# The first load of a batched matrix product, taken in three loads of 2, 2 and 4 rows per partition

## Chip, cores and metric

The kernel runs on one core of one Trainium2 chip. The metric is the time of one execution in microseconds (us), as the device measures it. It is some 1.8 us longer than the span of the profile, which runs from the first to the last instruction.

## The reference

32 products of a 256 x 512 matrix with a 512 x 384 matrix, in float32:

```python
x: (32, 256, 512) float32      y: (32, 512, 384) float32
np.einsum('bij,bjk->bik', x, y)    # (32, 256, 384) float32
```

That is 41.94 MB to read and 12.58 MB to write.

## The kernel before

A load of x brings four batches (a "q") at once: 32 partitions per batch and eight neighbouring rows of x on each partition, so 16 KB in one piece per partition. A unit (a "u") is two batches; its y comes in two loads with 6 KB per partition. All loads and stores are issued by SP, in the order of the program.

```python
    def load_x(q):                                    # P = 128, R = 8 rows, J = 512
        x_of[q] = x_pool.tile([P, R, J], F32, name="x_sb")
        keep(nc.sync.dma_start(
            out=x_of[q],
            in_=x[q * Q : (q + 1) * Q].rearrange("g (p r) j -> (g p) r j", r=R)))

    def transpose(q, half):
        ...
        for t in range(half * NJ // 2, (half + 1) * NJ // 2):     # NJ = 4
            for e in range(0, NE, 2):                             # NE = 4
                t_ps = tpsum_pool.tile([P, 2, H, Q * PQ], F32, name="t_ps")
                for f in range(2):
                    for h in range(H):                            # H = 2
                        keep(nc.tensor.transpose(
                            t_ps[:, f, h], x_sb[:, h * NE + e + f, t::NJ], identity))
                ...                                   # DVE and ACT in turn round t_ps to float16

    for s in range(U + 2):                            # U = 16 units
        if s + ahead < U:
            load(s + ahead)                           # ahead = 2; unit 0 and 1 are loaded before the loop
        if s == 0:
            transpose(0, 0); transpose(0, 1)
        if s >= 2:
            collect(s - 2)                            # PSUM -> SBUF
        if 1 <= s <= U:
            multiply(s - 1)                           # 32 matmuls
        if s < U:
            round_y(s)                                # y to float16
        ...                                           # the transposes of later x, in halves
        if s >= 2:
            store(s - 2)
```

The first tile t_ps takes row 0 and then row 4 of each partition (`h * NE + e + f`), then rows 1 and 5.

Of the kernel before, what the change touches and what calls it, by code (L numbers as in the profile page):

```python
# [1 line left out]

# [5 lines left out]


MM_DT = mybir.dt.float16  # L10
F32 = mybir.dt.float32
P = 128


Q = 4
G = 2

LAG = 4


@with_exitstack
def kernel(
    ctx: ExitStack,
    tc: tile.TileContext,
    x: bass.AP,
    y: bass.AP,
    out: bass.AP,
):
    nc = tc.nc

    B, I, J = x.shape
    _, _, K = y.shape


    M = P // G
    NE = I // M
    NJ = J // P



    PQ = P // Q
    R = I // PQ
    H = R // NE
    U = B // G

    const_pool = ctx.enter_context(tc.tile_pool(name="const", bufs=1))
    x_pool = ctx.enter_context(tc.tile_pool(name="x_pool", bufs=3))
    y_pool = ctx.enter_context(tc.tile_pool(name="y_pool", bufs=5))
    yr_pool = ctx.enter_context(tc.tile_pool(name="yr_pool", bufs=2))
    xt_pool = ctx.enter_context(tc.tile_pool(name="xt_pool", bufs=2))  # L50
    o_pool = ctx.enter_context(tc.tile_pool(name="o_pool", bufs=5))
    tpsum_pool = ctx.enter_context(tc.tile_pool(name="tpsum", bufs=4, space=bass.MemoryType.PSUM))
    opsum_pool = ctx.enter_context(tc.tile_pool(name="opsum", bufs=4, space=bass.MemoryType.PSUM))


    keep = tc.keep_in_program_order

    identity = const_pool.tile([P, P], F32)
    make_identity(nc, identity)

    x_of, y_of, yr_of, xt_of, ps_of, o_of = {}, {}, {}, {}, {}, {}

    def load_x(q):
        x_of[q] = x_pool.tile([P, R, J], F32, name="x_sb")
        keep(
            nc.sync.dma_start(
                out=x_of[q],
                in_=x[q * Q : (q + 1) * Q].rearrange("g (p r) j -> (g p) r j", r=R),
            )
        )  # L70

    def load(u):

        if u == 0:
            load_x(0)
        if (u + 1) * G % Q == 0 and u + 1 < U:
            load_x((u + 1) * G // Q)
        y_of[u] = y_pool.tile([P, G, NJ, K], F32, name="y_sb")
        for g in range(G):
            keep(  # L80
                nc.sync.dma_start(
                    out=y_of[u][:, g],
                    in_=y[u * G + g].rearrange("(q t) k -> q t k", q=P),
                )
            )

    def transpose(q, half):

        x_sb = x_of[q]
        if half == 0:  # L90
            xt_of[q] = xt_pool.tile([P, NJ, NE, Q * PQ, H], MM_DT, name="xt_sb")
        n = 0
        for t in range(half * NJ // 2, (half + 1) * NJ // 2):
            for e in range(0, NE, 2):
                t_ps = tpsum_pool.tile([P, 2, H, Q * PQ], F32, name="t_ps")
                for f in range(2):
                    for h in range(H):
                        keep(
                            nc.tensor.transpose(  # L99
                                t_ps[:, f, h], x_sb[:, h * NE + e + f, t::NJ], identity  # L100
                            )
                        )
                dst = xt_of[q][:, t, e : e + 2].rearrange("c f p h -> c f h p")
                if n % 2 == 0:
                    keep(nc.vector.tensor_copy(dst, t_ps))  # L105
                else:
                    keep(nc.scalar.copy(dst, t_ps))  # L107
                n += 1

    def round_y(u):  # L110
        y_sb = y_of.pop(u)
        yr_of[u] = yr_pool.tile([P, G, NJ, K], MM_DT, name="y_r")
        for g in range(G):
            for t in range(NJ):
                if t % 2 == 0:
                    keep(nc.scalar.copy(yr_of[u][:, g, t], y_sb[:, g, t]))  # L116
                else:
                    keep(nc.vector.tensor_copy(yr_of[u][:, g, t], y_sb[:, g, t]))  # L118

    def multiply(u):  # L120
        xt_sb, y_r = xt_of[u * G // Q], yr_of.pop(u)
        ps_of[u] = []
        for e in range(NE):
            o_ps = opsum_pool.tile([P, K], F32, name="o_ps")
            ps_of[u].append(o_ps)
            for t in range(NJ):
                for g in range(G):
                    a = (u * G + g) % Q
                    keep(
                        nc.tensor.matmul(  # L130
                            o_ps[g * M : (g + 1) * M],
                            xt_sb[:, t, e, a * PQ : (a + 1) * PQ].rearrange("c p h -> c (p h)"),
                            y_r[:, g, t],
                            start=(t == 0),
                            stop=(t == NJ - 1),
                        )
                    )

    def collect(u):
        o_of[u] = o_pool.tile([P, NE, K], F32, name="o_sb")  # L140
        for e in range(NE):
            if e % 2 == 0:
                keep(nc.scalar.copy(o_of[u][:, e], ps_of[u][e]))  # L143
            else:
                keep(nc.vector.tensor_copy(o_of[u][:, e], ps_of[u][e]))  # L145
        del ps_of[u]

    def store(u):
        keep(
            nc.sync.dma_start(  # L150
                out=out[u * G : (u + 1) * G].rearrange("g (m e) k -> (g m) e k", e=NE),
                in_=o_of.pop(u),
            )
        )


    ahead = LAG - 2
    for u in range(ahead):
        load(u)
    for s in range(U + 2):  # L160
        if s + ahead < U:
            load(s + ahead)
        if s == 0:
            transpose(0, 0)
            transpose(0, 1)
        if s >= 2:
            collect(s - 2)
        if 1 <= s <= U:
            multiply(s - 1)
        if s < U:  # L170
            round_y(s)
        for half in range(2):
            q = (s + 1 - half) * G // Q
            if (s + 1 - half) * G % Q == 0 and 0 < q < B // Q:
                transpose(q, half)
        if s >= 2:
            store(s - 2)


# [1 line left out]
_INS = ['x', 'y']  # L181
_OUTS = [((32, 256, 384), 'float32')]


# [23 lines left out]
```

## Time and profile before

| | before |
|---|---|
| time | 136.07 us (median of 3; 135.93 to 136.09) |
| span of the profile | 134.3 us |
| busy: PE, ACT, DVE | 66%, 48%, 42% of the span |
| transfers | 56: 8 of x, 32 of y, 16 of the output |
| mean rate | 406 GB/s over the span, 422 in the steady part |
| first transposes, first multiply, first store issued | 8.72, 15.91, 23.92 us |

The prediction below shows the slices and the chain. Here are the page's lines on transfers (DMA): how many packets, their sizes, and the queues that they came from with packets, MB and share of the 16 DMA engines' time.

```profile
DMA packets 8073, 54.65 MB, mean 407 GB/s; under 512 B 896, under 2 KB 896, under 8 KB 7040
q1 hardware_dynamic: 8064, 54.53, 97.8%
q8 instruction: 6, 0.10, 0.3%
q14 instruction: 3, 0.02, 0.0%
```

Queue q1 is the kernel's own loads and stores and fills 97.8% of the engines' time. The two queues called "instruction" I take for reads of the program itself: where `pool_fetch` below adds 1024 instructions, eight more reads of 8 KB stand there. They are 0.3% in all.

### The profile page before, as it was taken

Reading aid. Unit: us, or ns where it says so; the run is one execution under the profiler, and the core shown is the slowest. Engines: PE = TensorE matmul, PEld = TensorE weight load, DVE = VectorE, ACT = ScalarE, POOL = GpSimd, SP = SyncE. Lnnn points to the kernel's source line nnn. Section 1 sums busy time; section 2 is a strip of 40 time slices with the busy share of each in tenths; the row PEclk is TensorE's granted clock in tenths of the full one; section 3 lists DMA queues with packets and bytes.
Section 4 is the critical chain, followed back from the end, with each engine's and each line's share of the span. In section 5 each row is a group of like instructions: output and inputs, shape, how many; then the busy total and the mean of one; then the engine's idle time right before and its main releaser. Section 6 shows DMA issues by size and latency. Waiting matters only on the chain.

```text
span 134.3 us, 1968 instructions
## 1 busy us (share of the span) xinstructions
PE 88.5 (66%) x768; PEld 73.2 (55%) x768; DVE 56.2 (42%) x128; ACT 63.9 (48%) x129; POOL 0.7 (1%) x6
## 2 busy tenths in 40 slices
PE   0049494979299767786099771976439986597920
PEld 0049474768177666666078661864427665476810
DVE  0004717471743365711634318460363425628620
ACT  3004837662762476712744428560475336738610
POOL 2000000000000000000000000000000000000000
PEclk9999999999959999999968999999965899779997
DMA  5999999999999999999999999999999999999993
GB/s 112 415 400 450 409 417 421 456 388 421 417 448 408 409 428 421 457 394 417 413 443 436 408 417 428 442 422 402 425 423 444 426 402 427 419 427 419 417 394 158
DMA packets 8073, 54.65 MB, mean 407 GB/s; under 512 B 896, under 2 KB 896, under 8 KB 7040
## 3 DMA queue, kind: packets, MB, share of 16 engines
q1 hardware_dynamic: 8064, 54.53, 97.8%
q8 instruction: 6, 0.10, 0.3%
q14 instruction: 3, 0.02, 0.0%
HBM read 41.94 MB, written 12.58 MB: 406 GB/s over the span
## 4 chain that ended last, share of the span: by engine, by line
DMA 78%; PE 13%; ACT 4%; DVE 0%; issue 0%
DMA y_sb<-in_y_dram 40%; DMA x_sb<-in_x_dram 38%; PE o_ps L130 9%; PE t_ps L99 3%; ACT xt_sb L107 2%; ACT y_r L116 1%; ACT o_sb L143 1%; DVE o_sb L145 0%
## 5 line engine op out<-in xcount | busy, mean ns | idle before, releaser
L130 PE MATMUL o_ps<-y_r,xt_sb 128*64 128x384 f16 x512 | 52.4, 364 | 28.5 <-ACT o_sb L143 20.8
L130 PEld LDWEIGHTS <-xt_sb 128*64 128x64 f16 x512 | 39.1, 121 | 38.8 <-issue 22.4
L116 ACT CAST y_r<-y_sb 128x384 f16<-128x384 f32 x64 | 29.5, 514 | 38.7 <-DMA y_sb<-in_y_dram 38.6
L99 PE MATMUL t_ps<-identity,x_sb 128*128 128x128 f32 x256 | 36.9, 301 | 11.4 <-DMA x_sb<-in_x_dram 11.4
L99 PEld LDWEIGHTS t_ps<-identity,x_sb 128*128 128x128 f32 x256 | 34.1, 211 | 16.0 <-issue 16.0
L118 DVE CAST y_r<-y_sb 128x384 f16<-128x384 f32 x64 | 20.0, 356 | 46.7 <-DMA y_sb<-in_y_dram 46.7
L107 ACT CAST xt_sb<-t_ps 128x512 f16<-128x512 f32 x32 | 22.4, 731 | 23.6 <-PE t_ps L99 23.6
L105 DVE CAST xt_sb<-t_ps 128x512 f16<-128x512 f32 x32 | 22.6, 728 | 24.1 <-PE t_ps L99 23.8
L145 DVE COPY o_sb<-o_ps 128x384 f32<-128x384 f32 x32 | 16.3, 544 | 2.1 <-PE o_ps L130 2.1
L143 ACT COPY o_sb<-o_ps 128x384 f32<-128x384 f32 x32 | 13.9, 492 | 1.3 <-PE o_ps L130 1.3
L107 ACT ACT_TABLE_LOAD x1 | 1.3, 1283 | 0.7 <-PEq L192 0.7
masks.py:199 POOL TENSOR_SCALAR_AFFINE_SELECT identity<-identity 128x128 f32<-128x128 f32 x1 | 0.3, 294 | 0.1
masks.py:197 POOL MEMSET identity<- 128x128 f32 x1 | 0.2, 206 | 0.3 <-POOLq L192 0.3
L192 POOL MEMSET const-bfloat16-1.0<- 128x1 bf16 x1 | 0.1, 102 | 0.0
L192 POOL MEMSET const-uint8-127<- 128x1 uint8 x1 | 0.1, 102 | 0.0
L192 POOL MEMSET const-float32-0.0<- 128x1 f32 x1 | 0.1, 99 | 0.2 <-issue 0.2
L192 POOL MEMSET const-float32-1.0<- 128x1 f32 x1 | 0.1, 99 | 0.0
## 6 DMA issues: line engine op xcount, KB each, us to landing
y_sb<-in_y_dram SPq DMA_DIRECT2D x32, 768.0 KB, 17.9
x_sb<-in_x_dram SPq DMA_DIRECT2D x8, 2048.0 KB, 20.8
out_dram<-o_sb SPq DMA_DIRECT2D x16, 768.0 KB, 17.8
```

Source lines behind the costliest of these rows:

```text
L99: nc.tensor.transpose(t_ps[:, f, h], x_sb[:, h * NE + e + f, t::NJ], identity)
L105: keep(nc.vector.tensor_copy(dst, t_ps))
L107: keep(nc.scalar.copy(dst, t_ps))
L116: keep(nc.scalar.copy(yr_of[u][:, g, t], y_sb[:, g, t]))
L118: keep(nc.vector.tensor_copy(yr_of[u][:, g, t], y_sb[:, g, t]))
L130: nc.tensor.matmul(o_ps[g * M : (g + 1) * M], xt_sb[:, t, e, a * PQ : (a + 1) * PQ].rearrange("c p h -> c (p h)"), y_r[:, g, t], start=(t ...
L143: keep(nc.scalar.copy(o_of[u][:, e], ps_of[u][e]))
L145: keep(nc.vector.tensor_copy(o_of[u][:, e], ps_of[u][e]))
L192: nc = _bacc.Bacc("TRN2", target_bir_lowering=False, num_devices=1)
```

## The change

The intent: transposes of the first rows can start while the later rows still arrive.

```diff
+FIRST = (0, 2, 4, 8)
 ...
     def load_x(q):
         x_of[q] = x_pool.tile([P, R, J], F32, name="x_sb")
-        keep(nc.sync.dma_start(
-            out=x_of[q],
-            in_=x[q * Q : (q + 1) * Q].rearrange("g (p r) j -> (g p) r j", r=R)))
+        src = x[q * Q : (q + 1) * Q].rearrange("g (p r) j -> (g p) r j", r=R)
+        cuts = FIRST if q == 0 else (0, R)
+        for k, r in enumerate(cuts[:-1]):
+            rows = slice(r, cuts[k + 1])
+            keep(nc.sync.dma_start(out=x_of[q][:, rows], in_=src[:, rows]))
```

More of the change, by code (lines that the diff above doesn't have):

```diff
@@ L64, in load_x @@
         x_of[q] = x_pool.tile([P, R, J], F32, name="x_sb")
-        keep(
-            nc.sync.dma_start(
-                out=x_of[q],
-                in_=x[q * Q : (q + 1) * Q].rearrange("g (p r) j -> (g p) r j", r=R),
-            )
-        )
+        src = x[q * Q : (q + 1) * Q].rearrange("g (p r) j -> (g p) r j", r=R)
[3 more added lines that the diff above has]
+            keep(nc.sync.dma_start(out=x_of[q][:, rows], in_=src[:, rows]))
     def load(u):
```

## The prediction

Passages of the prediction, and one of the expectation of `pool_fetch`, that rested on what no run of this case shows are cut, and the cuts are marked. The sum of the prediction came to +0.1 us. Its one term other than zero, +0.1 us for the 18 added packets of each engine, is among the cuts, so the line of the sum stands without the estimate behind it.

> **What bounds the kernel now.** I read the page's slices first, then the chain that ended last, then windows of 16 us, then the order of events on the load-issuing engine and on the compute engines in the first 30 us and the last 20 us. The slices show that transfers never pause:
>
> ```profile
> PE   0049494979299767786099771976439986597920
> DMA  5999999999999999999999999999999999999993
> HBM read 41.94 MB, written 12.58 MB: 406 GB/s over the span
> ```
>
> The DMA engines are full (9) in 38 slices of 40, while PE is at 66% of the span and DVE and ACT are under 50%. The chain that ended last agrees: DMA has 78% of it and PE 13%. The steady rate comes from the windows (columns: length, four busy engines and POOL, granted clock, DMA share, GB/s):
>
> ```profile
> 24.40:40.40 16.00, 12.47 (x113) 10.20 (x110) 7.57 (x18) 8.98 (x19) 0.00 (x0) 0.90 1.00 419
> 56.40:72.40 16.00, 10.00 (x85) 8.05 (x86) 5.68 (x15) 6.96 (x15) 0.00 (x0) 0.89 1.02 424
> 88.40:104.40 16.00, 9.98 (x80) 7.59 (x80) 5.72 (x15) 7.01 (x15) 0.00 (x0) 0.82 1.02 426
> ```
>
> The six windows from 24.4 to 120.4 us show 419, 423, 424, 425, 426 and 416 GB/s, a mean of 422. The kernel's 54.53 MB at that rate take 129.2 us. The span is 134.3 us, so only 5.1 us are not steady streaming. Most of that is the start: two-microsecond windows show 98 and 213 GB/s up to 4 us, so 0.62 MB, worth 1.5 us; about 2.5 us are lost there. At the end, after 132 us, nearly nothing moves (59 GB/s), about 2.0 us lost to the landing of the last store. The rest is 0.35 us of lower rate between 128 and 132 us (381 and 390 GB/s) and some 0.2 us between 4 and 8 us.
>
> The start on the compute side, which the change aims at:
>
> ```profile
> 8.60 0.33 SPq L66 DMA_DIRECT2D x_sb<-in_x_dram  x1
> 8.72 6.00 PE L99 MATMUL t_ps<-identity,x_sb 128*128 128x128 f32 x32 [8.72 <-DMA x_sb<-in_x_dram]
> 15.91 0.32 PE L130 MATMUL o_ps<-y_r,xt_sb 128*64 128x384 f16 x1 [1.19 <-ACT y_r L116]
> 19.15 0.63 DVE L118 CAST y_r<-y_sb 128x384 f16<-128x384 f32 x2 [3.11 <-DMA y_sb<-in_y_dram]
> 21.04 0.63 DVE L118 CAST y_r<-y_sb 128x384 f16<-128x384 f32 x2 [1.25 <-DMA y_sb<-in_y_dram]
> 23.92 0.35 SPq L150 DMA_DIRECT2D out_dram<-o_sb  x1
> ```
>
> PE waits 8.7 us for the first load, transposes for 6.0 us, multiplies from 15.9 us, and then DVE idles 3.11 us until the second unit's y lands at 19.15 and 21.04 us. That landing, not the first transposes, holds back what follows. At the end:
>
> ```profile
> 115.54 4.47 PE o_ps L130 x32
> 120.02 2.15 PE t_ps L99 x16
> 122.16 0.02 issue
> 122.19 0.74 ACT xt_sb L107
> 122.92 0.09 issue
> 123.01 5.41 PE o_ps L130 x64
> 128.42 0.02 issue
> 128.44 0.56 DVE o_sb L145
> ```
>
> The last 64 matmuls end at 128.4 us, the last store is issued at about 129.1 and takes 4.4 us (the shortest landing of a store). The store queue is almost empty by then. So the end is both things at once: the stream of transfers, and a compute tail that starts from the last loads. Both hang on when the loads arrive.
>
> [...] 896 packets are under 512 B, and 56 transfers times 16 are 896.
>
> **The change part by part.** The first 2 MB load becomes three: rows 0-1 (0.52 MB), rows 2-3 (0.52 MB) and rows 4-7 (1.05 MB) of each partition. All bytes, all arithmetic and the order of the transfers stay.
>
> Packets: the page counts 8064 in the queue: 896 semaphore writes, 6144 of 6 KB (48 y loads and stores times 128) and so 1024 for the eight x loads, 128 of 16 KB each. The first load then has 3 times 128, which is 256 more, and 32 more semaphore writes: 288 more, 18 per engine. [...]
>
> Issue time: an issue of a load takes 0.33 to 0.63 us on the issuing engine. Two more, at about 0.4 us, end the third piece's issue near 2.0 us instead of 1.1 and push the next by about 0.8 us. By 4 us only 0.62 MB have moved, so the first piece still keeps the engines occupied when the others are queued: hidden, 0 us.
>
> Waits of the issuing engine: in the built kernel each transfer from the ninth on waits for the one eight places earlier. Every later transfer and the one it waits for shift by two places alike, so those waits stay the same, with the third piece in the place of the whole load. Only the two y loads of the third unit, which waited for nothing (they were among the four issues from 2.78 to 4.82 us), now wait for the first and second pieces. From the cumulated GB/s, 0.52 MB have moved by about 3.7 us and 1.05 MB by about 5.0; the whole load's 2.10 MB are reached at 7.7 and it landed at 8.6, so add 0.9: landings near 4.6 and 5.9 us. Those y loads follow 7.34 MB in the queue, whose turn ends near 2.5 + 7.34/0.422 = 19.9 us. The later issue has over 13 us of slack: 0 us.
>
> Compute: the built order on PE keeps its 32 transposes in the same order and gives the first a wait for piece one, the second a wait for piece three, and the fifth one for piece two. This is because a transposed tile takes row e+f and row 4+e+f together, so row 4 is needed second. So one transpose of 32 can run early, near 4.6 us; the other 31 start near 8.6 to 8.8 as before. It saves at most one mean transpose, 0.30 us, up to the first multiply. That 0.3 us then ends in the 3.11 us of DVE idling before 19.15 us. The first store at 23.92 us comes from results that stand in DVE's and ACT's order behind the rounding of the y that lands at 21.04. Worth 0 us at the end.
>
> Sum: +0.1 - 0 = +0.1 us, so 136.07 becomes about 136.15 us.
>
> **The rivals.** First, the intended one: transposes run as rows arrive and the pipeline starts some 4 us earlier. Against it is the wait of the second transpose for the third piece. Even if the rows were in a helpful order, the first multiply needs y of unit 0, which lands about 10.5 and 12.3 us, and the second unit's y at 21.04 would swallow the rest. Its gain: 0 us; 136.1. If the whole wait passed through to the end it would be 132, which I rule out while the DMA row reads 9.
>
> Second, the ramp of the stream. The first 4 us lose 2.5 us, and I can't see why the window at 2 to 3 us has a DMA share of only 0.64. Smaller first packets could fill that hole earlier, or three small issues could open another bubble. Nothing in the trace decides it. I allow 0.4 us either way: 135.7 to 136.5.
>
> Third, the tail and the clock. The granted clock is 0.50 from 116 to 119 us; the 32 matmuls there took 4.47 us, against 2.79 us for such a group at full clock. A shifted start could move these slow stretches. If the slow stretch missed the tail, compute would end up to 1.7 us earlier, but the stream has only its 0.35 us of lower rate to give: 135.7. If it fell on the last 64 matmuls, up to 1.7 us would be added: 137.8, which is 1.3%. For: such stretches come at 38, 69, 99 to 105 and 116 us. Against: the three timed runs agree to 0.16 us, and PE's load is unchanged.
>
> **Range and chances.** The centre is 136.15. The ramp gives 0.4 us either way, the tail adds a little more upwards, and noise is 0.1: 135.7 to 136.7. Faster by 2% would need 133.3 us, which is below even the 129.2 us of streaming plus the 4.5 us of start and landing: 0.01. Slower by 2% needs 138.8, more than the worst tail: 0.01. Within 2%: 0.98.
>
> **What would show it.** Right: first transpose near 4.6 us, then an idle of PE until about 8.7 us for the second; first multiply between 15.6 and 16.0; the second unit's y at about 19.2 and 21.1 us; first store near 23.9; 8352 packets in the queue; 422 GB/s in steady windows; the DMA row unchanged. Wrong: most transposes before 8 us, the y loads of the second unit landing over 0.5 us earlier or later than 21.04 (then the ramp rival holds), a hole in the DMA row in the first 20 us, or the last matmul more than 1 us away from 128.4 while loads land as before (the tail rival).

## The result

| | before | after |
|---|---|---|
| median of 6 runs each | 136.03 us (135.93 to 136.13) | 136.45 us (136.23 to 136.66) |
| ratio | | 1.003, interval 1.0017 to 1.0043 |

Ratios here are the mean time of one kernel's runs over that of the other's in the same rounds, so they are not quite the ratio of the medians. The change costs about 0.4 us, 0.3%. That is inside the range of the prediction, and four times the 0.1 us that its sum gave.

The page of the changed kernel, the same lines as before:

```profile
PE   0149491979297917978099792978539793597920
DMA  4999999999999999999999999999999999999992
HBM read 41.94 MB, written 12.58 MB: 404 GB/s over the span
q1 hardware_dynamic: 8352, 54.53, 97.3%
```

The queue has 8352 packets, 288 more, as counted beforehand. The DMA row is as full as it was. Two of the windows that stand in the prediction, now of the changed kernel (same columns):

```profile
24.40:40.40 16.00, 12.49 (x127) 10.50 (x124) 7.61 (x19) 9.07 (x20) 0.00 (x0) 1.00 1.01 420
88.40:104.40 16.00, 10.80 (x94) 8.80 (x92) 7.03 (x16) 7.83 (x16) 0.00 (x0) 0.89 1.01 424
```

The steady rate has not moved. The timeline of the start (columns: start, duration, engine and line, operation, operands, count, and in brackets the idle time before it with what ended it):

```profile
5.10 0.46 PE L100 MATMUL t_ps<-identity,x_sb 128*128 128x128 f32 x1 [5.10 <-DMA x_sb<-in_x_dram]
8.74 5.18 PE L100 MATMUL t_ps<-identity,x_sb 128*128 128x128 f32 x31 [3.17 <-DMA x_sb<-in_x_dram]
15.10 0.32 PE L131 MATMUL o_ps<-y_r,xt_sb 128*64 128x384 f16 x1 [1.19 <-ACT y_r L117]
19.25 0.63 DVE L119 CAST y_r<-y_sb 128x384 f16<-128x384 f32 x2 [4.02 <-DMA y_sb<-in_y_dram]
21.14 0.63 DVE L119 CAST y_r<-y_sb 128x384 f16<-128x384 f32 x2 [1.25 <-DMA y_sb<-in_y_dram]
24.02 0.35 SPq L151 DMA_DIRECT2D out_dram<-o_sb  x1
```

One transpose runs at 5.10 us, and the other 31 wait for the third piece and start at 8.74, where all 32 started at 8.72 before. The first multiply is 0.8 us earlier. DVE then idles 4.02 us instead of 3.11 until y of the second unit comes at 19.25 us, and the first store is issued at 24.02 instead of 23.92: the 0.8 us are gone there, and everything is 0.10 us late.

The chain at the end of the changed kernel:

```profile
116.15 4.17 PE o_ps L131 x32
120.33 2.29 PE t_ps L100 x16
122.62 0.02 issue
122.64 0.74 ACT xt_sb L108
123.38 0.09 issue
123.47 5.41 PE o_ps L131 x64
128.88 0.02 issue
128.90 0.56 DVE o_sb L146
```

The last matmuls end 0.46 us later than before, at 128.88. So the question is where 0.1 us at 24 us becomes 0.3 to 0.6 us at the end.

For that I used the landing records of the trace. A transfer's completion is counted 16 times (896 counts for the 56 transfers), which I take for one count by each of the 16 DMA engines, and each count has its time. The last of the 16 is what a waiting engine sees: the first load's came at 8.59 us, 0.62 us after its first, and SP went on at 8.60 and PE at 8.72 us. The difference from the first is how far the slowest DMA engine is behind the fastest. In the kernel before, this lag is 0.62 us at the first load, 1.55 us at 30.6 us, and between 1.65 and 2.0 us from 45 to 130 us. It grows in steps, and the first step, of 0.9 us, follows a program read of 16 KB at 27.3 us. The last three stores land at 129.69, 131.50 and 133.43 us. One store at 422 GB/s takes 1.86 us, so the slowest engine seems to work without a pause to the very end. (The records don't name the engines. That the slowest is the same one throughout is inferred from the steady lag.) In the changed kernel's first trace the lag steps from 2.04 to 2.58 us at 93.9 us, just after a program read at 87.6 us, and the last store lands at 133.88 us. That made two theories at first:

- **Packets:** the added packets and transfers delay the stream by some 0.15 us; the rest is chance, namely which DMA engine the program reads fall on.
- **Start:** the three short first loads leave the engines unevenly loaded, and this stays.

and beside them the prediction's rivals, the intended overlap and the **clock** of PE.

### The profile page after: what moved, and what is told of

It is laid out like the page before. It is cut to its first block, busy times and chain, and to the rows that moved or that the text cites. A ratio compares the mean times of both kernels' runs of the same rounds, so it can differ in the third digit from the quotient of the medians. Undisturbed runs are those within 1.5% of the kernel's fastest.

```text
span 134.9 us, 1970 instructions
## 1 busy us (share of the span) xinstructions
PE 89.1 (66%) x768; PEld 73.0 (54%) x768; DVE 56.3 (42%) x128; ACT 63.8 (47%) x129; POOL 0.7 (1%) x6
## 3 DMA queue, kind: packets, MB, share of 16 engines
q1 hardware_dynamic: 8352, 54.53, 97.3%
## 4 chain that ended last, share of the span: by engine, by line
DMA 77%; PE 12%; ACT 4%; SPq 1%; DVE 0%; issue 0%
DMA y_sb<-in_y_dram 40%; DMA x_sb<-in_x_dram 37%; PE o_ps L131 10%; ACT xt_sb L108 2%; PE t_ps L100 2%; ACT y_r L117 1%; SPq L71 1%; ACT o_sb L144 1%; DVE o_sb L146 0%
## 5 line engine op out<-in xcount | busy, mean ns | idle before, releaser
L131 PE MATMUL o_ps<-y_r,xt_sb 128*64 128x384 f16 x512 | 53.3, 368 | 31.1 <-ACT o_sb L144 23.4
L100 PEld LDWEIGHTS t_ps<-identity,x_sb 128*128 128x128 f32 x256 | 33.6, 211 | 14.1 <-issue 9.9
```

The source lines that it names most:

```text
L100: nc.tensor.transpose(t_ps[:, f, h], x_sb[:, h * NE + e + f, t::NJ], identity)
L131: nc.tensor.matmul(o_ps[g * M : (g + 1) * M], xt_sb[:, t, e, a * PQ : (a + 1) * PQ].rearrange("c p h -> c (p h)"), y_r[:, g, t], start=(t ...
```

## The experiments

All twelve runs were compared with the kernel before, run on the same chip in the same rounds: the first four kernels in one set (before: median 136.18 us, 11 runs), the next four in a second (136.09 us, 11 runs), the last four in a third (136.17 us, 11 runs). All results were correct except that of `no_wait`.

### null_before: the noise

No edit.

> The kernel before once more, unchanged. Every theory expects a ratio of 1.000 and about 136.03 us; the spread of its runs is the noise against which the 0.42 us of the change is read. In its trace the landing records show how far the slowest of the 16 DMA engines lies behind the first at each transfer: 1.3 us at the last store in the kernel before. If the lag is set by chance in each run (which engine an instruction read of 16 KB meets), the lags in the middle of the run should differ from those of the first trace by some 0.5 us.

Measured: 136.08 us (135.91 to 136.51), ratio 0.9993, interval 0.9972 to 1.0014. The lag of the slowest engine was 2.1 to 2.2 us from 67 to 128 us, where the first trace had 1.75 to 2.0, and it began at 1.02 us instead of 0.62. So the lag does differ from run to run of one kernel, by up to 0.4 us. The profiled run took 136.44 us. Its chain shows one cause of such runs:

```profile
115.79 5.31 PE o_ps L130 x32
124.08 5.41 PE o_ps L130 x64
```

The 32 matmuls took 5.31 us where the first trace has 4.47 (and 2.79 for such a group at a granted clock of 1.00, at 23.56 us), because the low clock (0.5 from 114.1 to 120.9 us, against 115.6 to 119.0 in the first trace) covered nearly all of them, and the last 64 started 1.07 us later. This time the last store landed 1.99 us after the one before it, a little over the 1.86 us of an unbroken stream: here compute held back the end by some 0.13 us.

### after_again and after_third: the size of the cost

No edit of the changed kernel.

> The changed kernel once more. Packet theory (each added packet costs its fixed time on its engine: 8.3 ns from a line through the packet durations 159, 234, 309 and 611 ns of 4, 6, 8 and 16 KB, 16 of them and two semaphore writes of 9 ns per engine, 0.15 us): 136.2 us, and the first trace, which is of the slowest of its six runs, was partly chance. Start theory (three short first loads leave the engines unevenly loaded, which lasts to the end): 136.45 again, with the slowest engine over 0.6 us further behind than before. Clock theory (the transposes start earlier and move the stretches of low clock): 136.45 again, with a granted clock lower than the kernel before has.

> The changed kernel a third time, on this chip, for the size of its cost. From the mean packet durations of all_cut past the start (4 KB 164.8 ns, 8 KB 315.4, against 617.8 for 16 KB in the kernel before): 0.24 us a cut, 136.3 to 136.35. If the cost is the fixed packet time alone: 136.2. If it is specific to this kernel and not to the packets: 136.45.

Measured: 136.42 us both times (136.37 to 136.68 and 136.34 to 137.15), ratios 1.0020 (1.0003 to 1.0036) and 1.0026 (1.0006 to 1.0045). With the first 1.0030, the mean is 1.0025, or 0.34 us. The cost is small but there in all three sets. The lag at mid-run was 2.2 to 2.3 us in both traces, not 2.6 as in the first, so the step at 93.9 us of the first trace was chance. The clock was 0.919 and 0.908.

### late_cut: the same cut in mid-stream

The edit is shown against the changed kernel.

```diff
-        cuts = FIRST if q == 0 else (0, R)
+        cuts = FIRST if q == 4 else (0, R)
```

> The same cut into three loads, made in the fifth load of x instead of the first: the same 18 added packets per engine, but in mid-stream with a full queue, and nothing different in the first 40 us. Packet theory: +0.15 us, so about 136.2, the same as for the changed kernel less what the start costs. Start theory: 136.05, no change. Clock theory: 136.05, no change.

Measured: 136.46 us (136.26 to 136.94), ratio 1.0023 (1.0003 to 1.0043), 0.31 us. The same cost without any change in the first 40 us. This speaks against the start theory, which expected none; with `after_again`, whose slowest engine was not over 0.6 us further behind, that theory falls. One set of six runs is weak evidence for 0.3 us by itself, though, as `warm_pe` below shows: the interval goes from 0.04 to 0.59 us. The clock theory falls for this kernel too, as PE's start is untouched. But 0.31 is also twice the packet theory's 0.15.

### by_partition: three first loads with unchanged packets

Against the kernel before; the removed load is the one shown under "The change".

```diff
+FIRST = (0, 32, 64, 128)
...
+        cuts = FIRST if q == 0 else (0, P)
+        for k, r in enumerate(cuts[:-1]):
+            part = slice(r, cuts[k + 1])
+            keep(nc.sync.dma_start(out=x_of[q][part], in_=x[q * Q : (q + 1) * Q].rearrange("g (p r) j -> (g p) r j", r=R)[part]))
```

> The first load in three, but by partitions (32, 32 and 64 of them) instead of rows: the packets stay at 16 KB, and only two semaphore writes per engine and two issues are added; all transposes wait for all three. Packet theory: +0.02 us, 136.05. Start theory: like the changed kernel, 136.4, as the first loads are as short and as many. Clock theory: 136.05, since no transpose starts early.

Measured: 140.59 us (140.43 to 140.75), ratio 1.0322. No theory expected that. The page's slices and the start of the transposes:

```profile
GB/s 151 227 227 257 428 423 411 420 480 372 415 415 457 393 420 425 441 428 403 426 413 458 409 409 425 422 447 402 418 423 436 438 399 425 425 423 422 418 396 133
12.66 6.08 PE L99 MATMUL t_ps<-identity,x_sb 128*128 128x128 f32 x32 [12.66 <-DMA x_sb<-in_x_dram]
```

The first slices, up to the landing of the third piece, run at about half the rate, 227 GB/s, though the page's DMA row reads 6, 9, 9 and 7 there: a 16 KB packet took about 1,270 ns instead of 611. Why these three loads ran at half the rate is not shown. As a test of the packet theory the run failed, since the edit brought in a large cost of its own. It shows something else: the first load lands 3.94 us later (12.53 instead of 8.59 us) and the kernel takes 4.4 us longer (0.165 us of it in the closing checks, shown below). A delay of the stream at the start reaches the end in full.

### all_cut: eight cuts instead of one

The edit is shown against the changed kernel.

```diff
-        cuts = FIRST if q == 0 else (0, R)
+        cuts = FIRST
```

> All eight loads of x cut into 2, 2 and 4 rows, so eight times the added packets: 128 data packets and 16 semaphore writes per engine. Packet theory: 8 x 0.15 = 1.2 us, 137.3. If each cut costs the 0.3 us that the single cuts measured, at the start and in mid-stream, it is 2.4 us, 138.5. Start theory: as the changed kernel, 136.45.

Measured: 137.94 us (137.48 to 138.79), ratio 1.0134 (1.0108 to 1.0159), 1.82 us, or 0.23 us a cut. That lies between the two expectations: more than 0.15 a cut, less than 0.3. Whatever the single cut costs beyond its packets does not come eight times. The trace also has one accident: at 107.6 us the lag of the slowest engine steps from 2.38 to 3.01 us, next to two program reads: one of 16 KB at 105.2 us, which the kernel before has at 104.8 with a step of 0.2 us at most, and one of 8 KB at 106.0 us, which the kernel before has at 132.6 us, after nearly all the work.

### all_pad: packets alone, many of them

```diff
-        x_of[q] = x_pool.tile([P, R, J], F32, name="x_sb")
+        x_of[q] = x_pool.tile([P, R, J + 16], F32, name="x_sb")
-                out=x_of[q],
+                out=x_of[q][:, :, :J],
...
-                                t_ps[:, f, h], x_sb[:, h * NE + e + f, t::NJ], identity
+                                t_ps[:, f, h], x_sb[:, h * NE + e + f, t:J:NJ], identity
```

> The kernel before with 64 bytes of padding after each row of x in SBUF, so each of the eight x loads moves 1024 packets of 2 KB instead of 128 of 16 KB, with no added transfer, issue or wait. 7168 more packets, 448 per engine. Fixed cost alone (8.3 ns from the line through the packet durations): +3.7 us, 139.8. At 13 ns a packet, which all_cut's 1.85 us over 144 added packets an engine gives: +5.8 us, 141.9. If added packets cost nothing and the cost of all_cut came from its added transfers: 136.1.

Measured: 139.28 us (139.22 to 139.77), ratio 1.0237 (1.0215 to 1.0260), 3.2 us. The page's line of the queue:

```profile
q1 hardware_dynamic: 15232, 54.53, 98.7%
```

15232 packets are 7168 more than 8064, 448 on each of the 16 engines, so 7.2 ns each (3.2 us / 448), with no transfer added. Added packets do cost, and they cost somewhat less than the 8.3 ns expected from their durations.

### ordered: an overlap that the row order allows

```diff
...                                                   # only for q 0; src is the x of the four batches
+            frm = src.rearrange("p (h e) j -> p h e j", h=H)
+            x_of[q] = [first_pool.tile([P, H, 2, J], F32, name=f"x_first{e}") for e in range(2)]
+            for e in range(2):                        # rows 0, 1, 4, 5 and then rows 2, 3, 6, 7
+                keep(nc.sync.dma_start(out=x_of[q][e], in_=frm[:, :, 2 * e : 2 * e + 2]))
...                                                   # for q 0, transposes in the order of the pieces
```

> The overlap that the change wanted, made to work: the first load in two pieces of 1 MB in tiles of their own, the first with rows 0, 1, 4 and 5, the second with rows 2, 3, 6 and 7, so that half of the first 32 transposes need the first piece alone, and they run in that order. The first transposes should start near 6.2 us instead of 8.7, in a whole group, and the first multiply some 1.5 to 2 us earlier than 15.9. Theory that the stream sets the time: no gain, but the cost of 24 added packets and one semaphore write per engine, 0.2 us: 136.3. Theory that the change only failed because of its row order: a gain of 1 us or more, 135 or less.

Measured: 138.14 us (137.99 to 138.34), ratio 1.0144 (1.0127 to 1.0161), 2.0 us slower. It doesn't decide what it was made for: the first piece landed at 7.92 us and not near 6.2, so the transposes began only 0.66 us earlier. The line of the timeline, and the rate by slices:

```profile
8.06 6.42 PE L107 MATMUL t_ps<-identity,x_first 128*128 128x128 f32 x32 [8.06 <-DMA x_first<-in_x_dram]
GB/s 66 253 418 454 432 393 416 449 400 410 422 445 426 399 423 422 456 400 411 419 436 446 398 427 422 447 422 405 418 427 445 414 414 429 420 422 429 380 326 186
```

The second slice has 253 GB/s where the kernel before has 415; 52 of the 512 packets of 4 KB took 0.35 to 1.34 us, where 0.159 is the median. Why this pattern starts so slowly stays open. Both pieces had landed 1.86 us later than the whole load did before (10.45 against 8.59 us), and the end moved by about that. It is a second case of a start delay that reaches the end in full.

### no_wait: the most that the intent could give

```diff
-                                t_ps[:, f, h], x_sb[:, h * NE + e + f, t::NJ], identity
+                                t_ps[:, f, h],
+                                identity if q == 0 else x_sb[:, h * NE + e + f, t::NJ],
+                                identity,
```

> The most that the change could ever give: the first 32 transposes read the identity instead of x, so they wait for no load at all and run from about 1.3 us (the result of the first four batches is wrong on purpose; all loads, the first one too, are as before). The first multiply then waits for y of the first unit alone, near 13.5 us instead of 15.9. Theory that the stream of transfers sets the end: 136.1, within 0.3 us of the kernel before, and the first store still near 23.9 us. Theory that the change only failed because rows 0 and 4 lie in different pieces: 2 us or more faster, 134 or less.

Measured: 136.15 us (136.01 to 136.42), ratio 0.9999 (0.9985 to 1.0013). Nothing at all, with the first transposes free of any wait. From the timeline of the start:

```profile
12.88 5.26 PE L132 MATMUL o_ps<-y_r,xt_sb 128*64 128x384 f16 x31 [1.53 <-ACT y_r L118]
20.98 0.63 DVE L120 CAST y_r<-y_sb 128x384 f16<-128x384 f32 x2 [1.25 <-DMA y_sb<-in_y_dram]
23.86 0.35 SPq L152 DMA_DIRECT2D out_dram<-o_sb  x1
```

The multiplies of the first unit start at 12.88 us, 3.8 us earlier than the same group before (16.73), but the second unit's y still lands at 20.98 and the first store is issued at 23.86 us. So the overlap is worth nothing here, whatever the row order. This run also speaks against the clock: its granted clock was 0.88 to 0.90 in all six runs, lower than in most others, at an unchanged time.

### warm_pe and warm_again: earlier work on PE

```diff
+    for _ in range(10):
+        w_ps = tpsum_pool.tile([P, 2, H, Q * PQ], F32, name="t_ps")
+        keep(nc.tensor.transpose(w_ps[:, 0, 0], identity, identity))
```

> The kernel before with ten transposes of the identity ahead of the first load's transposes: PE works from about 1.3 us, transfers are the same. Clock theory (earlier PE work moves the stretches of low clock and these set the end): 136.4 or another change clear of noise. Packet theory: 136.1, no change, since the slowest DMA engine sets the end.

> The kernel with ten early transposes once more, since its first +0.3 us is barely clear of noise. Clock theory: +0.3 again, with the low-clock stretches at the same places as the first time. Theory that its slowest engine was hit by three instruction reads by chance: between 136.0 and 136.4, and a lag of the slowest engine in mid-run that differs from the 2.8 us of the first trace.

Measured: 136.41 us (136.17 to 136.79), ratio 1.0021 (1.0003 to 1.0039) the first time, and 136.05 us (135.87 to 136.56), ratio 0.9995 (0.9978 to 1.0012) the second time. The two differ by more than either interval would suggest, so an effect of 0.3 us in one set of six runs is not safe by itself. The lag of the slowest engine was 2.8 us in the first trace and 2.0 in the second: the first had two steps in its slowest engine's lag, to 2.0 us at 26 us and to 2.9 at 46 us, the second had only one, to 2.0 us at 31 us. The clock theory, which expected the same gain or loss twice, falls.

### pool_fetch: more program to read

```diff
+    dots = const_pool.tile([1, 16], F32)
+    for n in range(1024):
+        nc.gpsimd.memset(dots[:, n % 16 : n % 16 + 1], 0.0)
```

> The kernel before with 1024 tiny memsets on the otherwise idle GpSimd: no more data, but more program to read, and the trace should show added instruction reads of 16 KB beside the six of before, each some 1.04 us on one DMA engine. If the end is set by the slowest engine and instruction reads are what makes it slow, the lag of the slowest engine grows and the time rises by 0.5 to 2 us (136.6 to 138). If instruction reads cost nothing at the end: 136.1. [...]

Measured: 139.88 us (139.35 to 140.06), ratio 1.0266 (1.0245 to 1.0287), 3.6 us slower, above the upper end of the expectation. From its page and the groups by line: the slices of the DMA engines, the queue of program reads, and DVE's roundings of y (busy us, mean ns, idle before):

```profile
DMA  5999999999999999999999999999999999996665
q14 instruction: 11, 0.09, 0.2%
L118 DVE CAST y_r<-y_sb 128x384 f16<-128x384 f32 x64 | 20.1, 359 | 47.0 <-DMA y_sb<-in_y_dram 47.0
```

There are 11 reads in q14 instead of 3: eight more, of 8 KB each and not 16 as in q8, about 5 us apart from 6.6 to 41.1 us. Together they are 0.07 MB, 0.1% of the bytes. But the landing records fit reads that all fall on one engine: its lag goes from 1.08 us in seven steps of 0.5 to 0.7 us to 5.4 us at 43.7 us, every time away from the second slowest, and stays there. In the other thirteen traces the lag grew by 0.5 to 1.3 us after the first read of 16 KB. The last four slices show the result: 6, 6, 6, 5 where the kernel before has 9, 9, 9, 3. The other engines have gaps while the slowest one still has its share of each transfer. DVE's copies are as long as before (359 against 356 ns), so slower copies don't explain it. This shows that one slow engine of the 16 moves the end, and that program reads can make it slow. It does so by way of the last loads: the last load landed at 127.75 us instead of 124.12, 3.63 us later, and the last store 3.77 us later. That store itself was issued only at 133.57 us, after a wait for DVE, and landed 2.10 us after the one before it with its sixteen landings only 0.55 us apart, so the last 0.2 us of this trace are compute.

### What all fourteen traces show of the end

One part of the cost was still missing, and it was in the traces all along. Each transfer signals one of eight semaphores in turn (112 counts on each in the kernel before, so seven transfers of 16 counts), and at the end SP checks all eight in an order that is fixed in the program, in five instructions of two semaphores each (the other two belong to compute engines). These are records of the trace and not a view of the profile: start and duration in us of SP's semaphore instructions after the last store was issued.

```
before (56 transfers)          after (58 transfers)
129.83  0.03                   129.94  0.03
129.91  0.03                   130.01  3.90   waits for the last store
129.98  0.03                   133.94  0.03
131.52  0.03                   134.01  0.03
133.45  0.03   last store      134.07  0.03
133.51  first drain            134.14  first drain
```

Before, the last store uses the semaphore that is checked last, and 0.08 us after its landing SP goes on. With two more transfers the turn of semaphores is shifted by two. The last store's semaphore is now checked early, and three more checks, some 0.06 us each, come after the wait, so that SP goes on 0.25 us after the landing. The profile shows it only as two waits of SP that became one (total, count and longest in us; before and after):

```profile
SPq L203 <- DMA out_dram<-o_sb: 3.4, 2, 1.9
```

```profile
SPq L204 <- DMA out_dram<-o_sb: 3.9, 1, 3.9
```

From the landing of the last transfer to the end of the span, over all traces:

| kernel | transfers | first x landed, us | last store landed, us | end of span, us | from landing to end, us |
|---|---|---|---|---|---|
| before | 56 | 8.59 | 133.43 | 134.27 | 0.835 |
| null_before | 56 | 8.78 | 133.74 | 134.58 | 0.834 |
| no_wait | 56 | 8.54 | 133.51 | 134.35 | 0.841 |
| warm_pe | 56 | 8.57 | 134.10 | 134.93 | 0.834 |
| warm_again | 56 | 8.52 | 133.26 | 134.09 | 0.835 |
| pool_fetch | 56 | 8.76 | 137.20 | 138.03 | 0.834 |
| all_pad | 56 | 9.32 | 136.59 | 137.43 | 0.835 |
| all_cut | 72 | 8.70 | 135.40 | 136.23 | 0.829 |
| ordered | 57 | 10.45 | 135.44 | 136.39 | 0.944 |
| after | 58 | 8.69 | 133.88 | 134.88 | 1.000 |
| after_again | 58 | 8.81 | 133.65 | 134.65 | 1.000 |
| after_third | 58 | 8.83 | 133.56 | 134.56 | 1.001 |
| late_cut | 58 | 8.47 | 133.76 | 134.76 | 1.000 |
| by_partition | 58 | 12.53 | 137.71 | 138.71 | 1.000 |

The number in the last column sorts by the count of transfers and by nothing else in the table: 0.83 to 0.84 us where the count is a multiple of eight (56, 72), 1.00 us at 58. The difference is 0.165 us, the same in every trace with 58, and it doesn't depend on where the cut is made. That is how `late_cut` can cost as much as the change, and one reason why eight cuts, which come to 72 transfers, don't cost eight times as much.

One more thing moves with the cut by rows: the program's last read of 8 KB comes at 130.4 or 130.5 us in the four traces of the change and `late_cut`, and at 132.6 before. In none of the four does the distance of the slowest engine from the second slowest grow after it (by more than 0.01 us), so it adds nothing that these traces show.

## Why the prediction was right, and its sum too small

**What bounds the kernel: held.** I wrote that the end is both the stream of transfers and a compute tail, and that the store queue is almost empty by then. The engines on average were near an empty queue, but the slowest one was not: its last three stores landed 1.8 to 1.9 us apart. A slow DMA engine moves the end (`pool_fetch`, by 3.6 us). In three of the fourteen traces (`null_before`, `ordered`, `pool_fetch`) the compute after the last loads also held it back: the last store came 2.0 to 2.1 us after the one before it instead of 1.86, with its sixteen landings only 0.5 us apart.

**Compute: held, with one size off.** One transpose ran early and the other 31 at 8.74 us, for the reason given (row 4 in the third piece). I allowed it 0.30 us, but the first multiply came 0.8 us earlier, as the 31 transposes took 5.18 us where all 32 had taken 6.00 (why is not shown). This went where the prediction said, into the wait for y of the second unit. `no_wait` shows that even 3.8 us would have gone there, so the first rival's value of 0 us holds as measured, not only as argued.

**Issues and waits of SP: held for the stream.** The pieces landed at 4.96, 6.19 and 8.69 us (predicted near 4.6, 5.9 and 8.6), and no hole opened in the DMA row. What I left out was the end of the same engine's program.

**Packets: right in kind, but 0.1 us was too little.** From the durations in the trace, 16 packets of 159 ns, 8 of 309 and two semaphore writes of 9 in place of 8 packets of 611 come to 2544 + 2472 + 18 - 4888 = 146 ns on each engine, 8.1 ns for each of the 18 added; `all_pad` measured 7.2 ns on many. The mistake was not to take the cost from durations of packets when two of them stood in the trace of the kernel before (234 ns for 6 KB and 611 for 16 KB; the line through both leaves some 7.8 ns for each packet, whatever its size): the 0.1 us was my estimate, and it rested in part on a figure that no run shows. In five traces of kernels with the first load uncut and its compute rearranged or not (before, `null_before`, `no_wait`, `warm_pe`, `warm_again`) it landed at 8.60 us on average (8.52 to 8.78), in the three of the changed kernel at 8.78 (8.69 to 8.83): 0.18 us, but the ranges overlap. The bytes moved separate them better: by 24 us the queue's packets had carried 8.91 to 8.94 MB in the three traces of the changed kernel, and 8.97 to 9.01 MB in those five and `late_cut`. The difference of the means, 0.06 MB, is 0.15 us at 422 GB/s.

**The step that failed is "Sum: +0.1 - 0 = +0.1 us".** It lacks one term and has another too small. The stream's part is 0.15 to 0.18 us instead of 0.1, and the closing checks add 0.165 us. Together they are 0.31 to 0.35 us, and the mean ratio of three sets gives 0.34 us. `late_cut` comes to 0.146 + 0.165 = 0.31 and measured 0.31. The intervals of the single sets reach some 0.2 to 0.3 us to either side, so the match to a hundredth is chance: the first set of the change (0.23 to 0.58 us) excludes the 0.1 us of the prediction, and the other two and `late_cut` only just contain it. That the result lay in the range is partly luck: the range was made wide for the ramp and for the tail, and the missing 0.2 us or so came from neither. In the traced runs by themselves the last store lands only 0.1 us later on average (133.70 in three against 133.61 in five), but single traces of one kernel differ by up to 0.8 us, so this average can't tell 0.1 from 0.2. For `all_cut` the sum is 8 x 0.146 = 1.17 us; the 0.65 us left would fit the step of 0.63 us at the 8 KB program read, but I have not shown that every run of it has that step, nor which of the two reads there made it.

**The ramp and the clock.** The ramp rival had room for 0.4 us either way and used little of it: by the windows of 1 us, 0.50 MB had moved by 4 us instead of 0.62, but 2.63 MB instead of 2.64 by 9 us. The tail rival was right that low-clock stretches shift from run to run and move the end by tenths (`null_before`), and wrong as an effect of this change: `warm_again` and `no_wait` move PE's work and not the time.

**What stays open.** I read the cost of the closing checks from fourteen traces (`all_cut`, with cuts and 72 transfers, doesn't have it) and did not test it by a kernel with, say, 56 or 64 transfers and one cut. What decides on which DMA engine a program read falls, why `by_partition` loads at half the rate, and why `ordered` starts slowly, is not settled. No variant beat the kernel before.

## What to carry to other kernels

An earlier start of compute was worth nothing here (3.8 us earlier in `no_wait`, ratio 0.9999), where the transfers are the bound and the next load is what compute waits for; ask first which arrival swallows the gain, and test it by letting the work start without any wait. In this stream, which never pauses, the slowest DMA engine decided when the last loads arrived and so moved the end (`pool_fetch`: 5.4 us behind, the last load 3.63 us later, the last store 3.77), so look at the spread of a transfer's sixteen landings and at what else uses those engines, not only at the mean rate. A part of a change of a few tenths of a microsecond came from the last instructions of the program here (0.165 us of 0.34), namely the order in which transfers are waited for, so compare the time from the last landing to the end as well.
